# A hybrid RG-LRU/S5 decoder layer on one core: one PSUM bank is skipped behind the gates of the LRU stage

## Chip, core and metric

The kernel runs on one core of one Trainium2 chip. The metric is device time in microseconds (us), the median of the runs shown; lower is better. Beside it stands one profiled execution, from which all durations below come. The engines are named as in the profile: PE is TensorE, ACT is ScalarE, DVE is VectorE, POOL is GpSimd, SP issues the DMAs.

## The reference, cut to what matters

One layer works on 1024 prompt positions and 8 sequences of 4 sample positions, 1056 columns in all, with 1024 features. The part around the change is the recurrent branch:

```python
z = u @ w_in + b_in
z_lru, z_gate, z_s5, m_a, m_b = jnp.split(z, SPLITS, axis=-1)
v, conv_new = causal_conv(z_lru, conv0, w_conv, b_conv)
...
g = jnp.einsum('bthi,ghij->gbthj', vb, w_gates).reshape(2, Bn, T, D_RNN)
gates = jax.nn.sigmoid(g.astype(jnp.float32) + b_gates.astype(jnp.float32)[:, None, None, :])
r, i = gates[0], gates[1]
log_a = -LRU_C * r * jax.nn.softplus(-lam.astype(jnp.float32))
a = jnp.exp(log_a)
bterm = jnp.sqrt(-jnp.expm1(2.0 * log_a)) * (i * v.astype(jnp.float32))
_, h = lax.associative_scan(_lin_op, (a, bterm), axis=1)
br_a = (h.astype(dt) * jax.nn.gelu(z_gate)) @ w_lru_out
```

Before it lie the conditioning (ada) and the S5 branch, behind it the weight GLU, the output product, two layer norms and a SwiGLU.

## The kernel before

Activations are held with features on the 128 partitions and the 1056 columns in three blocks of 352. Every float32 product is made of three TensorE products of rounded high and low halves (high by high, high by low, low by high), so one block of 128 output features over 1024 inputs is 24 matmuls. The order of the work is written out by hand: each engine executes its instructions in the order in which the code issues them, and `later(n, fn)` puts a step n blocks (`tick()`) further on.

**The LRU stage** is the loop `for j in range(8)` behind `conv_bias()`. I call its iterations passes. Pass j does, on PE, in this order:

- block 0 of z_lru for feature tile j (`zl_block(w, j, 0)`, matmul line L997),
- from pass 1 on, the gates of tile j-1 (`lru_gates`, matmul line L1043): six outputs, for each of three blocks one for gate r and one for gate i, three matmuls each,
- blocks 1 and 2 of z_lru for tile j (L997),
- three blocks of z_gate for tile j-1 (`product(... zg_evac)`, matmul line L344),
- one part of the ada product (`ada_job`, L403) and, after each fourth part, its small selecting product (`ada_sel4`, L413).

Each result leaves PSUM as follows. A z_lru block is scaled by ACT (L1002) and then read three more times by DVE, which adds the other three taps of the convolution straight from PSUM (L126, `scalar_tensor_tensor`). A gate leaves by one ACT tanh (L1044). A z_gate block leaves by two ACT instructions (L1034, L1035).

The rest of the recurrence runs on DVE, ACT and POOL beside the products: `lru_0` to `lru_3` (tanh L1050, exp L1051, sqrt L1057 on ACT; the scan L1071 on DVE), `lru_out` (gelu with the tanh L1080 on ACT), the split into high and low halves of v (`lru_split`: ACT L1027, DVE L117) and of the result (`lru_hi_lo`: ACT L1086, POOL L117). A pass of ACT begins, in this document, with the L1027 of block 2: it waits for DVE's sample convolution (`lru_conv`).

**The banks.** PSUM has eight banks of 512 columns. In this stage `banks[0]` is 7: bank 7 is kept for the ada product, and `bank()` hands out the other seven in turn:

```python
    def bank():
        b = bank_at[0] % banks[0]
        bank_at[0] += 1
        return ps[:, b]
```

A pass takes twelve: block 0 of z_lru, six gates, blocks 1 and 2 of z_lru, three blocks of z_gate. If block 0 has bank s, the gates have s+1 to s+6, and block 1 is given s again: a product into a bank begins when the last reader of what it held is done. Block 2 is given the first gate's bank, and the z_gate blocks those of gates 2, 3 and 4.

After the loop come the last gates in the same way: one block of the last merge gate (`blocks(w, e, 0, 1)`), the gates of tile 7, an `ada_job`, three blocks of z_gate for tile 7 (the first one in the bank of that merge block), and two more merge blocks. The following stages, which open with `lr.close()`, load their operands anew and go on with the same turn of seven banks, later six.

Of the kernel before, what the change touches and what calls it, by code (L numbers as in the profile page):

```python
# [71 lines left out]
def tile_hawk_s5(ctx: ExitStack, tc: tile.TileContext, io):  # L72
# [46 lines left out]
    def ts(e, out, a, s0, s1=None, op0=OP.mult, op1=OP.add):  # L119
        if s1 is None:  # L120
            e.tensor_scalar(out, a, s0, None, op0=op0)
        else:
            e.tensor_scalar(out, a, s0, s1, op0=op0, op1=op1)

    def stt(e, out, a, s, b, op0, op1):
        e.scalar_tensor_tensor(out, a, s, b, op0=op0, op1=op1)  # L126
# [68 lines left out]
# [4 lines that stand above are left out]
# [839 lines left out]
    def lru_gates(j):  # L1038
        for nb in range(3):
            for g, dst in ((0, t_e), (1, t_f)):  # L1040
                b = bank()
                for q, (w, v) in enumerate(((gwh, vhr), (gwl, vhr), (gwh, vlr))):
                    PE.matmul(b[:, :NB], w[:, g, :], v[:, nb], start=q == 0, stop=q == 2)  # L1043
                A.activation(dst[:, 352 * nb:352 * nb + 352], b[:, :NB], AF.Tanh,  # L1044
                             bias=bgh[:, g, j:j + 1], scale=0.5)

    def lru_0(j):

        stt(V, t_f, t_f, 1.0, t_bb[j % 2], OP.add, OP.mult)
        A.activation(t_c, t_e, AF.Tanh, bias=sp2[:, j:j + 1], scale=sp2[:, j:j + 1])  # L1050
        A.activation(t_e, t_e, AF.Exp, bias=sp4[:, j:j + 1], scale=sp4[:, j:j + 1])  # L1051
        ts(V, t_e, t_e, 1.0, op0=OP.add)
# [43 lines left out]
    def gates_and_on(j):  # L1096
        lru_gates(j)
        for n, fn in ((1, lru_0), (2, lru_1), (3, lru_2), (5, lru_3)):
            later(n, fn, j)
        if j < 7:  # L1100
            later(2, gate_split, j + 1)
# [831 lines left out]
```

## Time and profile before

| | |
|---|---|
| time, median of 3 runs | 1794.03 us (1792.05 to 1795.2) |
| the profiled execution's own time | 1794.15 us |
| its span, first to last instruction | 1792.4 us |
| PE busy | 1719.7 us, 96% of the span |
| DVE busy | 1101.9 us, 61% |
| POOL busy | 882.0 us, 49% |
| ACT busy | 716.2 us, 40% |
| mean granted clock of TensorE | 0.982 of full speed |

How to read it: time and span differ by 1.75 us, which lie around the first and the last instruction. A busy share is an average over stages of different kinds; PE's idle time is spread over a few places, and the view of waits names them. The LRU stage runs from about 358 to about 640 us of the span. "idle before <-releaser" is the time that an engine stood still before an instruction and the line whose end let it go on. [...]

### The profile page before, as it was taken

The numbers are of one execution on the slowest core, as the hardware profiler recorded it, in microseconds if no ns is written. First come the engines' busy times: TensorE is split into PE (matmuls) and PEld (weight loads), VectorE is DVE, ScalarE is ACT, GpSimd is POOL, SyncE is SP. The second block draws the span as 40 slices with busy tenths as digits, with TensorE's granted clock in tenths as the row PEclk, the third lists the DMA queues.
The fourth block names the chain that finished last, engine by engine and source line by source line (L and its number), as shares of the span: only waits on it lengthen the run. The fifth ranks groups of instructions, "written<-read, shape, count | busy, mean of one in ns | idle before, by whom it ended". The sixth has DMA issues, their size and how long they took to land.

```text
span 1792.4 us, 33919 instructions
## 1 busy us (share of the span) xinstructions
PE 1719.7 (96%) x13380; PEld 1685.8 (94%) x13380; DVE 1101.9 (61%) x2026; ACT 716.2 (40%) x1456; POOL 882.0 (49%) x744
## 2 busy tenths in 40 slices
PE   6999999999898999999999998999999999999996
PEld 5989999998898999999999998999999998999996
DVE  6989999457687733322785685345554454533587
ACT  4533334346556633223354364344433333211244
POOL 3454343124344322355678616577767775222654
PEclk9999999999899999999999999999999999999999
DMA  9345555431112168665344323333322236832211
GB/s 358 89 123 154 177 152 168 132 106 63 50 42 74 36 183 241 220 224 188 113 155 158 111 96 118 108 124 120 116 96 96 102 115 250 335 125 76 81 37 61
DMA packets 118639, 240.93 MB, mean 134 GB/s; under 512 B 23120, under 2 KB 62288, under 8 KB 115408
## 3 DMA queue, kind: packets, MB, share of 16 engines
q1 hardware_dynamic: 118480, 238.76, 40.7%
q8 instruction: 105, 1.72, 0.4%
q14 instruction: 54, 0.44, 0.1%
HBM read 179.59 MB, written 54.97 MB: 131 GB/s over the span
## 4 chain that ended last, share of the span: by engine, by line
PE 76%; DVE 12%; DMA 4%; ACT 4%; POOL 3%; issue 2%; SPq 1%; POOLq 0%; DVEq 0%; ACTq 0%
PE ps L1206 36%; PE ps L344 19%; PE ps L1725 12%; PE ps L997 4%; DVE lru_t L126 3%; DVE rear_t L117 2%; DVE r_t L117 1%; DMA x_in_t<-in_x_dram 1%; POOL r_t L117 1%; POOL weights_t L117 1%; DVE lru_t L117 1%; DMA small_t<-in_w_down_dram 1%; DMA ada_w_t<-in_w_ada_dram 1%; DVE s_t L117 1%; PE ps L752 1%
## 5 line engine op out<-in xcount | busy, mean ns | idle before, releaser
L1206 PE MATMUL ps<-r_t,weights_t 128*128 128x264 f32 x5496 | 683.2, 285 | 10.9 <-POOL weights_t L117 7.4
L1206 PEld LDWEIGHTS ps<-r_t,weights_t 128*128 128x128 f32 x5496 | 672.5, 188 | 17.2 <-POOL weights_t L117 9.3
L117 POOL TENSOR_TENSOR weights_t<-small_t,weights_t 128x512 fp32r<-128x512 f32 (+3 forms) x312 | 390.8, 1268 | 494.7 <-ACT weights_t L232 436.8
L344 PE MATMUL ps<-r_t,weights_t 128*128 128x352 f32 x2808 | 469.7, 326 | 2.7 <-ACT weights_t L232 1.5
L344 PEld LDWEIGHTS ps<-r_t,weights_t 128*128 128x128 f32 x2808 | 453.2, 190 | 10.5 <-issue 6.1
L232 ACT ACTIVATE weights_t<-small_t 128x512 fp32r<-128x512 f32 (+3 forms) x286 | 151.5, 572 | 247.1 <-PE ps L1725 99.0
L1725 PE MATMUL ps<-r_t,weights_t 128*128 128x264 f32 x1344 | 166.6, 286 | 3.7 <-ACT weights_t L232 3.4
L1725 PEld LDWEIGHTS ps<-r_t,weights_t 128*128 128x128 f32 x1344 | 165.3, 190 | 4.9 <-ACT weights_t L232 3.6
L126 DVE SCALAR_TENSOR_TENSOR rear_t<-ps,small_t,rear_t 128x264 f32<-128x264 f32 (+1 forms) x192 | 92.4, 482 | 123.1 <-PE ps L1725 96.0
L117 DVE TENSOR_TENSOR small_t<-ps,small_t 128x264 f32<-128x264 f32 (+1 forms) x228 | 84.7, 378 | 102.0 <-ACT small_t L1650 74.4
L126 DVE SCALAR_TENSOR_TENSOR rear_t<-rear_t,ps 128x264 f32<-128x264 f32 (+1 forms) x74 | 33.1, 456 | 176.1 <-PE ps L1206 98.3
L997 PE MATMUL ps<-r_t,weights_t 128*128 128x356 f32 (+1 forms) x576 | 110.2, 356 | 21.3 <-DVE lru_t L126 21.3
L997 PEld LDWEIGHTS ps<-r_t,weights_t 128*128 128x128 f32 x576 | 106.2, 213 | 24.2 <-ACT lru_t L1050 22.7
L117 POOL TENSOR_TENSOR r_t<-rear_t,r_t 128x264 fp32r<-128x264 f32 (+2 forms) x77 | 96.7, 1259 | 60.9 <-ACT r_t L1221 24.1
L117 DVE TENSOR_TENSOR rear_t<-rear_t,small_t 128x32 f32<-128x32 f32 (+3 forms) x137 | 95.7, 707 | 41.0 <-POOL weights_t L117 30.9
L117 POOL TENSOR_TENSOR rear_t<-rear_t,small_t 128x264 f32<-128x264 f32 (+1 forms) x108 | 91.0, 865 | 54.6 <-ACT small_t L1269 44.3
L117 POOL TENSOR_TENSOR weights_t<-rear_t,weights_t 128x512 fp32r<-128x512 f32 x57 | 75.2, 1324 | 55.6 <-ACT weights_t L1566 55.5
L1725 PE MATMUL ps<-r_t 128*128 128x264 f32 x768 | 96.7, 286 | 0.8 <-POOL r_t L117 0.8
L1725 PEld LDWEIGHTS ps<-r_t 128*128 128x128 f32 x768 | 94.6, 188 | 1.7 <-POOL r_t L117 1.2
L117 POOL TENSOR_TENSOR r_t<-small_t,r_t 128x528 fp32r<-128x528 f32 (+1 forms) x58 | 78.7, 1368 | 35.3 <-ACT r_t L211 25.3
L117 DVE TENSOR_TENSOR s_t<-s_t 128x128 f32<-128x128 f32 (+4 forms) x184 | 74.7, 449 | 5.6 <-ACT s_t L700 3.2
L1206 PE MATMUL ps<-r_t 128*128 128x264 f32 x600 | 76.7, 283 | 0.0
(228 smaller groups left out, 1944.3 us busy)
## 6 DMA issues: line engine op xcount, KB each, us to landing
d_f<-r_t SPq DMA_DIRECT2D x44, 528.0 KB
r_t<-d_f SPq DMA_DIRECT2D x22, 1056.0 KB
small_t<-in_w_up_dram SPq DMA_DIRECT2D x43, 512.0 KB
small_t<-in_w_in_dram SPq DMA_DIRECT2D x40, 512.0 KB
small_t<-in_w_ada_dram SPq DMA_DIRECT2D x32, 512.0 KB
small_t<-in_w_glu_dram SPq DMA_DIRECT2D x32, 512.0 KB
ada_w_t<-in_w_ada_dram SPq DMA_DIRECT2D x16, 512.0 KB
small_t<-in_w_out_dram SPq DMA_DIRECT2D x16, 512.0 KB
```

Of the source, the lines that this page charges most:

```text
L117: e.tensor_tensor(out, a, b, op=op)
L126: e.scalar_tensor_tensor(out, a, s, b, op0=op0, op1=op1)
L232: A.activation(self.hi[:, s], self.raw[:, s], AF.Copy)
L344: PE.matmul(out[:, :NB], a[:, k, :], x[:, h, nb, k, :], start=bool(first and n == 0 and q == 0), stop=bool(last and n == len(kts) - 1 and ...
L752: PE.matmul(wb_[64 * h:64 * h + 64, 136 * n:136 * n + 136], wt[:, 2 * pr + h, 64 * r:64 * r + 64], ub[:, 2 * pr + h, 8:144], start=True, s ...
L997: PE.matmul(b[:, 4 - n:356], a[:, k, :], r1w[:, h, k, 352 * nb - n:352 * nb + 352], start=k == q == 0, stop=k == 7 and q == 2)
L1206: PE.matmul(out[:, :Q], a[:, k, :], x(h, k), start=bool(first and n == 0 and q == 0), stop=bool(last and n == len(kts) - 1 and q == 2), sk ...
L1725: PE.matmul(b[:, :Q], a[:, n, :], f[:, h, Q * q:Q * q + Q], start=n == i == 0, stop=k == k1 - 1 and i == 2)
```

## The change

One call is added at the end of `lru_gates`: a bank is taken from the turn and not used.

```diff
@@ -1044,6 +1044,8 @@
                 A.activation(dst[:, 352 * nb:352 * nb + 352], b[:, :NB], AF.Tanh,
                              bias=bgh[:, g, j:j + 1], scale=0.5)
 
+        bank()
+
     def lru_0(j):
```

No instruction is added, removed or moved on any engine; what changes is which bank an instruction writes and reads, and so what it waits for. `lru_gates` is called eight times. With block 0 of z_lru in bank s and the gates in s+1 to s+6, block 1 now has s+1 (the first gate's), block 2 s+2 (the second gate's), and the z_gate blocks those of gates 3, 4 and 5. The next pass begins at s+6, and its first gate takes s, the bank in which block 0 of the pass before stood.

PE, in pass 1 to 7 of the LRU stage, from the last gate's matmuls (L1043) to the second z_lru block (L997 with 356 columns); in brackets the engines whose semaphores an instruction waits for:

```order
 L1043 MATMUL ps<-r_t,lru_w_t 128x352 [waits Activation_49]
 L1043 MATMUL ps<-r_t,lru_w_t 128x352 x2
-L997 MATMUL ps<-r_t,weights_t 128x356 [waits DVE_49,Activation_49]
+L997 MATMUL ps<-r_t,weights_t 128x356 [waits Activation_49]
 L997 MATMUL ps<-r_t,weights_t 128x356 x23
 L997 MATMUL ps<-r_t,weights_t 128x356 [waits Activation_49]
```

The first matmul of block 1 no longer waits for DVE; it still waits for ACT.

PE again, in passes 2 and later, at the step from block 0 of z_lru to the first two gates:

```order
 L997 MATMUL ps<-r_t,weights_t 128x352 [waits Pool_49]
 L997 MATMUL ps<-r_t,weights_t 128x352 x9
-L1043 MATMUL ps<-r_t,lru_w_t 128x352
-L1043 MATMUL ps<-r_t,lru_w_t 128x352 [waits DVE_49]
+L1043 MATMUL ps<-r_t,lru_w_t 128x352 [waits DVE_49] x2
 L1043 MATMUL ps<-r_t,lru_w_t 128x352 x4
 L1043 MATMUL ps<-r_t,lru_w_t 128x352 [waits DVE_49,Activation_49]
```

The first gate's first matmul now waits for DVE's reads of block 0 of the pass before; it waited for nothing there.

## Rows read from the trace of the kernel before

**Rows 1.** View of waits of PE (us in total, times, longest us).
```profile
PE ps L997 <- DVE lru_t L126: 21.3, 6, 3.9
```

**Rows 2.** Windows: us, busy time (x instructions) by engine, PEclk, DMA share, GB/s.
```profile
381.76:408.58 26.82, 26.82 (x182) 26.34 (x178) 17.60 (x26) 15.79 (x30) 7.97 (x9) 1.00 0.24 85
...
385.69:396.45 10.76, 10.76 (x68) 10.70 (x67) 6.86 (x11) 8.18 (x12) 0.00 (x0) 1.00 0.27 111
412.51:427.51 15.00, 12.52 (x67) 12.26 (x67) 10.10 (x12) 9.36 (x14) 4.43 (x3) 0.89 0.15 48
443.57:460.68 17.11, 13.36 (x68) 13.10 (x67) 10.20 (x13) 10.39 (x15) 7.02 (x6) 0.80 0.12 36
476.74:494.42 17.68, 13.80 (x69) 13.71 (x69) 10.41 (x14) 10.54 (x15) 6.00 (x6) 0.81 0.11 36
510.48:526.66 16.18, 12.46 (x67) 12.19 (x67) 10.16 (x13) 10.36 (x15) 6.98 (x6) 0.89 0.12 39
542.72:559.75 17.03, 13.29 (x67) 13.03 (x67) 10.19 (x13) 10.38 (x15) 7.00 (x6) 0.80 0.12 39
575.81:593.31 17.50, 13.75 (x69) 13.49 (x67) 10.20 (x13) 10.38 (x15) 7.02 (x6) 0.80 0.12 36
```

**Rows 3.** Timeline of PE, passes 1, 3, 4 (start, us, engine, line, operation).
```profile
385.69 3.04 PE L1043 MATMUL ps<-r_t,lru_w_t 128*128 128x352 f32 x18
388.57 8.04 PE L997 MATMUL ps<-r_t,weights_t 128*128 128x356 f32 x48
...
443.57 3.04 PE L1043 MATMUL ps<-r_t,lru_w_t 128*128 128x352 f32 x18
450.37 10.47 PE L997 MATMUL ps<-r_t,weights_t 128*128 128x356 f32 x48 [3.75 <-DVE lru_t L126]
...
479.62 0.31 PE L413 MATMUL ps<-small_t 128*128 128x36 f32 x2
```

**Rows 4.** Windows, as in rows 2: behind a wait in pass 3, and behind LRU.
```profile
450.30:453.00 2.70, 2.63 (x9) 2.66 (x10) 1.91 (x3) 0.88 (x1) 0.00 (x0) 0.50 0.00 0
...
656.00:660.00 4.00, 2.87 (x16) 2.30 (x16) 0.00 (x0) 3.44 (x5) 2.54 (x2) 1.00 1.08 269
```

**Rows 5.** Timeline of ACT, DVE and POOL, from pass 3 to pass 4.
```profile
439.23 0.50 ACT L1027 ACTIVATE r_t<-lru_t 128x352 fp32r<-128x352 f32 x1 [5.14 <-DVE lru_t L126]
...
445.38 2.77 ACT L1044 ACTIVATE lru_t<-ps,small_t 128x352 f32<-128x352 f32 x6
...
448.42 1.80 DVE L126 SCALAR_TENSOR_TENSOR lru_t<-ps,small_t,lru_t 128x349 f32<-128x349 f32 x3
...
449.91 1.27 ACT L1051 ACTIVATE lru_t<-lru_t,small_t 128x1056 f32<-128x1056 f32 x1
...
450.34 1.25 DVE L126 SCALAR_TENSOR_TENSOR lru_t<-lru_t 128x1056 f32<-128x1056 f32 x1
...
451.51 0.70 DVE L121 TENSOR_SCALAR lru_t<-lru_t 128x1056 f32<-128x1056 f32 x1
456.95 0.65 ACT L1002 ACTIVATE lru_t<-ps,small_t 128x352 f32<-128x352 f32 x1 [5.77 <-PE ps L997]
...
457.63 1.83 DVE L126 SCALAR_TENSOR_TENSOR lru_t<-ps,small_t,lru_t 128x352 f32<-128x352 f32 x3 [5.42 <-ACT lru_t L1002]
...
458.65 2.47 POOL L117 TENSOR_TENSOR r_t<-lru_t,r_t 128x1056 fp32r<-128x1056 f32 x1 [10.09 <-ACT r_t L1086]
459.37 2.13 DVE L117 TENSOR_TENSOR r_t<-lru_t,r_t 128x352 fp32r<-128x352 f32 x1
...
472.38 0.50 ACT L1027 ACTIVATE r_t<-lru_t 128x352 fp32r<-128x352 f32 x1 [5.13 <-DVE lru_t L126]
```

**Rows 6.** Timeline of ACT, PE and DVE behind the loop.
```profile
611.05 2.77 ACT L1044 ACTIVATE lru_t<-ps,small_t 128x352 f32<-128x352 f32 x6
...
612.14 4.08 PE L344 MATMUL ps<-r_t,weights_t 128*128 128x352 f32 x24
...
632.79 0.53 DVE L126 SCALAR_TENSOR_TENSOR lru_t<-lru_t 128x352 f32<-128x352 f32 x1 [3.96 <-ACT lru_t L1080]
```

## The prediction

> **What bounds the kernel now.** I read the view of waits first. TensorE is busy almost throughout, so what matters is where it stands still. The largest entry is this stage's: matmuls of line 997 waited six times for DVE's line 126, 21.3 us in all, the longest wait 3.9 us [rows 1]. Line 997 is z_lru and line 126, with PSUM as a source, is the convolution: block 1 waits for the bank that DVE still reads block 0 from.
>
> Then I read the stage pass by pass, as windows from the first gate matmul to the first z_gate matmul, a stretch in which PE does the same 66 matmuls each time (18 of gates, 48 of z_lru). Pass 1 needs 10.76 us at full clock, passes 2 to 7 need 15.00 to 17.68 us [rows 2]. In the timeline of PE, pass 1 goes from its gates to block 1 in 2.88 us (385.69 to 388.57), pass 3 in 6.80 us (443.57 to 450.37), of which 3.75 us are the wait [rows 3]. The second loss is the clock. [...]
>
> Last I read the other engines in pass 3. DVE reads block 0 from 448.42 to 450.22 and PE starts block 1 at 450.37 [rows 3, 5]: the wait ends exactly there. The first gate's bank was free much earlier: the six gate tanhs begin at 445.38 and take 2.77 us, so the first ends at about 445.84 [rows 5].
>
> **What the change removes.** Block 1 of z_lru gets the bank of the first gate, and its first matmul loses its wait for DVE. PE can begin block 1 at 443.57 + 2.88 = 446.45, and in pass 3 the first gate's bank is free 0.6 us before that. So the wait goes, and with it the stop that precedes the low clock. The excess of each stretch over pass 1 is 4.24, 6.35, 6.92, 5.42, 6.27 and 6.74 us; 0.31 us of the third is the selecting product in that stretch [rows 2, 3], which stays. The sum is 35.6 us. Of it 21.3 us is idle time by the view of waits; the other 14.3 us is mostly matmuls at the lower clock. Pass 1 has nothing to lose, since DVE has no gelu of an earlier tile to do there.
>
> The other waits of the edit I cost at nothing. Block 2 takes the second gate's bank and the z_gate blocks those of gates 3 to 5. All six tanhs end at 448.15 [rows 5], over 2 us before block 2 could begin (446.45 + 4.0 = 450.5, with half of the 8.04 us of the two blocks [rows 3]). The first gate of a pass now waits for DVE's reads of block 0 of the pass before; in pass 3 they end at 450.22 and the gates of pass 4 start at 476.74 [rows 2, 5]. In the later stages only the phase of the turn moves, and their banks are reused in the same order. No DMA and no order changes.
>
> **What it adds.** PE's pass becomes 26.82 us [rows 2], and something else may no longer keep up. The chain through DVE and ACT goes round once a pass too: from ACT's first instruction of pass 3 to that of pass 4, 472.38 - 439.23 = 33.15 us [rows 5]. Part of that round is today's wait for PE: DVE ends lru_0 at 451.51 + 0.70 = 452.21 and stands still until block 1 arrives, at 457.63. With block 1 done at about 450.5, ACT can evict it as soon as its exp ends (449.91 + 1.27 = 451.18, and 0.65 us for the eviction), so DVE starts on it at 452.21, 5.42 us earlier. The round is then 33.15 - 5.42 = 27.7 us. It may be 0.3 us less: DVE's split of block 0 takes 2.13 us and ends 0.4 us after POOL's 2.47 us (458.65 to 461.12), and POOL starts 1.02 us after DVE's taps now, about 0.7 us after them when ACT has gone straight on. So the round is 27.4 to 27.7 us against PE's 26.8.
>
> So DVE and ACT fall behind by 0.6 to 0.9 us a pass, and PE meets it where its margin is least, at the first gate's eviction, the bank of block 1. I take pass 3 to begin with the margin of today, 0.6 us, since in pass 2 PE and the chain lose about the same stretch. Pass 4 has 0.0 to -0.3 us left, and its selecting product of 0.31 us covers that. Pass 5 waits 0.3 to 0.9 us, passes 6 and 7 what the round is too long, 0.6 to 0.9 us each. Behind the loop there is one such place more: the first z_gate block of tile 7 takes the first gate's bank, free at 611.05 + 0.46 = 611.51 and wanted at 612.14 [rows 6]; the lag makes it wait 0.7 to 1.0 us. The sum of the new waits is 2.2 to 3.7 us. Below, nothing is possible, if DVE and ACT run a little closer; I take 3.0 us, in the middle of the two, since the rows do not tell which of the two rounds holds. I charge no clock for these waits: at 656 to 660 us PE stood still for over a microsecond (2.87 us busy of 4.00) and the granted clock stayed at 1.00 [rows 4]. If each of the four did cost a slow stretch, its price is today's: the excess of a pass less its wait, at most 6.74 - 3.75 = 3.0 us, 12 us for four.
>
> What is late next, once this is gone, is the end of the stage on DVE: the last tile's gelu. There DVE waits 3.96 us for ACT before 632.79 us [rows 6], for merge blocks that PE itself has to produce first, so a lag of 1 to 2 us disappears. The loads of the next stage start when this one closes and move forward with it. I count the whole gain as reaching the end.
>
> **Sum.** 1794.15 (the profiled execution's own time, 0.1 us from the median 1794.03) - 35.6 + 3.0 = 1761.5 us.
>
> **Rivals.**
>
> - The wait goes and no new one comes: 1794.15 - 35.6 = 1758.5 us. For it: the 27.4 us round is near PE's 26.8, and part of DVE's stops beside POOL may fall otherwise.
> - The waits become short, but the clock still falls behind them: 1794.15 - 21.3 + 3.0 = 1775.9 us. Against it: the window at 656 to 660 us [rows 4], where the clock held. [...]
> - Slower. With PE no longer waiting, DVE's and POOL's work fall onto each other in another way, and the round of DVE and ACT grows instead of shrinking. It decides from a round longer than the 33.15 us of now [rows 5]; at 34 us the six passes lose 5 us and the time is 1799 us. For it: the split of block 0 takes 2.13 us beside POOL [rows 5]. Against it: 27.7 us would have to grow by 5.4 us, and the order of each engine's work does not change, so that DVE and POOL keep most of their places to each other.
> - The change does not do what it says, because something else in block 1 waits as long: 1794 us. Against it: its first matmul has only ACT left to wait for, and in pass 3 the six tanhs were done 2.2 us before block 1 began.
>
> **How the numbers follow.** My forecast, waits of 1.5 us to 6 us (1760 to 1764.5), has 0.62; no new waits 0.16; the clock rival with all between it and the forecast 0.15; no effect 0.03; slower 0.02; 0.02 is left for a later stage that takes something back or gives more. The range has to hold 8 in 10: I reach down to 1756 (1758.5 less the 2 us by which the runs scatter) and up to 1772, most of the way to the clock rival and near the 12 us bound. A measurement of this kernel tells about 0.2% (3.6 us) from no change: faster 0.95, within 0.03, slower 0.02.
>
> **What would show it.** Right: the wait of line 997 for DVE's line 126 gone from PE's waits; windows from first gate to first z_gate matmul near 10.8 us (11.1 in pass 4, up to 11.7 in passes 5 to 7) at a clock of 1.00; new small waits of line 997 for ACT's line 1044, under 1 us each; DVE's wait for block 1 gone and the round from one L1027 of block 2 to the next 27.4 to 27.7 us in passes 4 to 7. Wrong: such windows of over 13 us, a clock below 0.95 in them, a round above 29 us, or a gain in this stage that does not reach the end of the span.

## The result, and the profile after

| | before | after |
|---|---|---|
| median time | 1793.55 us (1792.05 to 1795.2, 4 runs) | 1760.55 us (1759.51 to 1761.71, 4 runs) |
| ratio | | 0.9819, 95% interval 0.9807 to 0.9831 |
| span of the profiled execution | 1792.4 us | 1757.7 us |
| PE / DVE busy | 1719.7 / 1101.9 us | 1704.9 / 1102.5 us |
| mean granted clock of TensorE (PEclk in the windows), share of full speed | 0.982 | 0.992 |

The forecast was 1761.5 us. (The kernel before has a fourth run here, hence 1793.55 us and not 1794.03.) DVE's work is the same; PE is busy for 15 us less with the same matmuls, and stands still for less.

The view of waits after the change, PE, 355 to 610 us (us in total, times, longest us). The entry of 21.3 us [rows 1] is gone:

```profile
PE ps L997 <- ACT lru_t L1044: 0.8, 3, 0.3
PE ps L344 <- ACT lru_t L1044: 0.4, 1, 0.4
```

The windows that answer to those of before [rows 2], from the first gate matmul to the first z_gate matmul of passes 1 to 7, after the change:

```profile
384.74:395.47 10.73, 10.73 (x67) 10.73 (x67) 6.85 (x11) 8.18 (x12) 0.00 (x0) 1.00 0.27 107
411.53:422.26 10.73, 10.73 (x67) 10.73 (x67) 10.11 (x12) 9.38 (x14) 4.44 (x3) 1.00 0.20 71
438.32:449.06 10.74, 10.74 (x69) 10.74 (x67) 9.26 (x13) 10.19 (x15) 6.52 (x6) 1.00 0.20 61
465.12:476.17 11.05, 11.05 (x70) 11.05 (x70) 9.40 (x13) 10.39 (x15) 5.54 (x6) 1.00 0.18 62
492.23:503.58 11.35, 11.03 (x68) 10.73 (x67) 9.87 (x13) 10.79 (x15) 7.13 (x6) 1.00 0.20 59
519.64:530.86 11.22, 11.00 (x68) 10.71 (x67) 9.74 (x13) 10.66 (x15) 7.00 (x6) 1.00 0.18 61
546.92:558.16 11.24, 10.98 (x67) 10.69 (x67) 9.76 (x13) 10.69 (x15) 7.03 (x6) 1.00 0.20 63
```

The granted clock is 1.00 in all seven, and passes 2 to 7 are within 0.62 us of pass 1. The timeline of ACT, DVE and POOL in pass 3, to hold against the one of before [rows 5]:

```profile
433.96 0.50 ACT L1027 ACTIVATE r_t<-lru_t 128x352 fp32r<-128x352 f32 x1 [5.13 <-DVE lru_t L126]
...
443.17 1.80 DVE L126 SCALAR_TENSOR_TENSOR lru_t<-ps,small_t,lru_t 128x349 f32<-128x349 f32 x3
...
445.85 0.63 ACT L1002 ACTIVATE lru_t<-ps,small_t 128x352 f32<-128x352 f32 x1
446.25 0.70 DVE L121 TENSOR_SCALAR lru_t<-lru_t 128x1056 f32<-128x1056 f32 x1
...
446.87 1.82 DVE L126 SCALAR_TENSOR_TENSOR lru_t<-ps,small_t,lru_t 128x352 f32<-128x352 f32 x3
...
447.53 2.48 POOL L117 TENSOR_TENSOR r_t<-lru_t,r_t 128x1056 fp32r<-128x1056 f32 x1 [4.22 <-ACT r_t L1088]
...
448.61 1.78 DVE L117 TENSOR_TENSOR r_t<-lru_t,r_t 128x352 fp32r<-128x352 f32 x1
...
461.28 0.50 ACT L1027 ACTIVATE r_t<-lru_t 128x352 fp32r<-128x352 f32 x1 [5.14 <-DVE lru_t L126]
```

DVE reads block 0 until 444.97, but PE began block 1 at 441.20 (438.32 + 2.88). DVE goes from lru_0 (446.25 + 0.70) to block 1 without a stop, where it stood still for 5.42 us [rows 5], and the round from one L1027 of block 2 to the next is 461.28 - 433.96 = 27.3 us instead of 33.15.

Two lines of PE before and two after bound the LRU stage, from its first z_lru block to the first block of the next product:

```profile
357.98 11.81 PE L997 MATMUL ps<-r_t,weights_t 128*128 128x352 f32 x72
...
640.01 11.71 PE L344 MATMUL ps<-r_t,weights_t 128*128 128x352 f32 x72
```

```profile
357.03 11.81 PE L997 MATMUL ps<-r_t,weights_t 128*128 128x352 f32 x72
...
605.23 11.72 PE L344 MATMUL ps<-r_t,weights_t 128*128 128x352 f32 x72
```

The stage took 282.0 us and takes 248.2: 33.8 us of the 34.7 us by which the span is shorter. The rest lies ahead of the stage (357.98 against 357.03), where nothing was changed; in the other runs' traces the stage begins between 356.75 and 359.04 us. Behind it both have 1152.4 to 1152.5 us left, so nothing is given back.

### The profile page after: what moved, and what is told of

It reads as the page before. It is cut to its first block, busy times and chain, and to the rows that moved or that the text cites. A ratio compares the mean times of both kernels' runs of the same rounds, so it can differ in the third digit from the quotient of the medians.

```text
span 1757.7 us, 33905 instructions
## 1 busy us (share of the span) xinstructions
PE 1704.9 (97%) x13380; PEld 1671.8 (95%) x13380; DVE 1102.5 (63%) x2026; ACT 715.3 (41%) x1456; POOL 883.9 (50%) x744
## 4 chain that ended last, share of the span: by engine, by line
PE 75%; DVE 13%; ACT 4%; POOL 3%; DMA 2%; issue 2%; SPq 0%; POOLq 0%; DVEq 0%; ACTq 0%
PE ps L1208 38%; PE ps L344 19%; PE ps L1727 12%; DVE lru_t L126 4%; PE ps L997 2%; DVE rear_t L117 1%; POOL weights_t L117 1%; POOL r_t L117 1%; DVE lru_t L117 1%; DVE r_t L117 1%; DVE s_t L117 1%; PE ps L752 1%; PE ps L822 1%; PE ps L821 1%; PE ps L403 1%
## 5 line engine op out<-in xcount | busy, mean ns | idle before, releaser
L1208 PEld LDWEIGHTS ps<-r_t,weights_t 128*128 128x128 f32 x5496 | 672.6, 188 | 16.8 <-POOL weights_t L117 10.5
L997 PE MATMUL ps<-r_t,weights_t 128*128 128x356 f32 (+1 forms) x576 | 97.0, 326 | 0.8 <-ACT lru_t L1044 0.8
L997 PEld LDWEIGHTS ps<-r_t,weights_t 128*128 128x128 f32 x576 | 93.2, 188 | 3.1 <-ACT lru_t L1044 1.7
```

Source lines behind the costliest of these rows:

```text
L997: PE.matmul(b[:, 4 - n:356], a[:, k, :], r1w[:, h, k, 352 * nb - n:352 * nb + 352], start=k == q == 0, stop=k == 7 and q == 2)
L1208: PE.matmul(out[:, :Q], a[:, k, :], x(h, k), start=bool(first and n == 0 and q == 0), stop=bool(last and n == len(kts) - 1 and q == 2), sk ...
```

## Experiments

Ratios are to the kernel before on the same chip, with their 95% interval. The change, experiments 1 to 4, 5 to 8, and 9 with 10 were measured in four sittings. The median of the kernel before moved by 2 us between them (from 1793.55 to 1791.46), so in experiments 4 to 8 a time set against the change's is good to that; experiments 9 and 10 are from one sitting.

**1. The same skip at another place.** From the kernel before:

```diff
         w = use_w("in", j)
+        if j:
+            bank()
         zl_block(w, j, 0)
...
+    bank()
     blocks(w, e, 0, 1)
     gates_and_on(7)
```

> From the kernel before, with the same eight skipped banks, but each one ahead of block 0 of z_lru (passes 1 to 7 and the merge block behind the loop) instead of behind the gates. The turn moves on as in the change, yet block 1 is back in block 0's bank. Theory (what counts is whose bank block 1 takes): no change, 1793.5 us within 3 us, line 997 waits 21 us for DVE's line 126, stretches from first gate to z_gate of 15 to 17.7 us. Rival (a turn of other length helps by itself, here or in the later stages): near 1760 us.

Measured: 1793.0 us, ratio 1.0006 (0.9997 to 1.0015). The wait of line 997 is that of before to a tenth:

```profile
PE ps L997 <- DVE lru_t L126: 21.3, 6, 3.9
```

A turn that moves on by thirteen does nothing by itself; a bank has to be skipped between the gates and block 1.

**2. The skip in four of seven passes.** From the change:

```diff
-        bank()
+        if j < 4:
+            bank()
```

> The change, but the bank is skipped only in passes 1 to 4 (gates of tiles 0 to 3). Theory (each pass has its own loss): passes 2 to 4 give back 4.2 + 6.4 + 6.6 = 17.2 us, passes 5 to 7 keep theirs, and the first of them waits about 0.9 us longer because DVE has fallen behind: 1777 us. Rival (one wait pushes DVE back for the rest of the loop, or the gain comes from the end of the loop): near 1760 or near 1793 us.

Measured: 1777.5 us, ratio 0.9916 (0.9901 to 0.9930). Windows of passes 5, 6, 7, and of pass 3:

```profile
494.18:511.25 17.07, 12.31 (x68) 12.05 (x67) 11.19 (x13) 11.40 (x15) 7.96 (x6) 0.90 0.12 37
527.31:543.59 16.28, 12.53 (x67) 12.27 (x67) 10.18 (x13) 10.38 (x15) 7.00 (x6) 0.90 0.12 40
559.65:575.87 16.22, 12.46 (x67) 12.20 (x67) 10.19 (x13) 10.38 (x15) 7.01 (x6) 0.89 0.12 38
440.33:451.06 10.73, 10.73 (x67) 10.73 (x67) 9.24 (x13) 10.18 (x15) 6.52 (x6) 1.00 0.20 60
```

Each pass loses for itself. The first one without the skip waits 4.75 us, about 0.9 us more than the others had before, which fits the lag of DVE behind PE that the expectation had put at that size.

**3. The wait filled with matmuls.** From the kernel before, behind the gates (`b0` is the first gate's bank):

```diff
+        for _ in range((0, 16, 23, 23, 23, 23, 23, 0)[j]):
+            PE.matmul(b0[:, :NB], gwh[:, 0, :], vhr[:, 0], start=True, stop=True)
```

> From the kernel before, without the skip: in passes 2 to 7, PE does 16 (pass 2) or 23 more matmuls behind the gates, into the first gate's bank, which nobody reads; they fill the time in which it waits for DVE. The wait stays as long, but PE does not stand still. Theory (14 us of the 35.6 are the low clock that follows the stop): stretches of 13.4 to 14.7 us at a granted clock of 1.00, time 1793.5 - 14 = 1779.5 us, within 2 us. Rival (the matmuls behind the wait are slow for another reason, such as DVE and ACT at work on PSUM): clock still 0.8 to 0.9 or matmuls still slow, 1793 us or more.

Measured: 1779.7 us, ratio 0.9931 (0.9917 to 0.9946). Windows of passes 2 and 3, and PE in pass 3:

```profile
411.74:425.12 13.38, 13.38 (x83) 13.26 (x83) 10.12 (x12) 9.37 (x14) 4.44 (x3) 1.00 0.17 56
441.18:455.88 14.70, 14.70 (x91) 14.42 (x90) 10.21 (x13) 10.38 (x15) 7.03 (x6) 1.00 0.17 60
```

```profile
444.06 3.84 PE L1049 MATMUL ps<-r_t,lru_w_t 128*128 128x352 f32 x23
447.90 8.15 PE L997 MATMUL ps<-r_t,weights_t 128*128 128x356 f32 x48
```

The 48 matmuls of blocks 1 and 2 take 8.15 us behind the filled wait, where they took 10.47 behind the empty one [rows 3], with ACT and DVE as busy as before, and the granted clock is 1.00 in both windows, where it was 0.89 and 0.80 [rows 2]. So the 35.6 us come apart: about 13 us was the low clock behind the stop, and some 22 us the stop, which the added matmuls only cover. More work on PE made the kernel 12.6 us faster.

**4. Block 1 in the last gate's bank.** From the change:

```diff
-        bank()
+        for _ in range(6):
+            bank()
```

> The change with six banks skipped instead of one: block 1 takes the last gate's bank, which ACT frees 2.3 us after the first gate's. Theory (block 1 begins when its bank is evicted, and PE and the round of DVE and ACT then hold each other up): pass 1 and 2 wait 0.8 to 0.9 us, pass 3 1.7 us, passes 4 to 7 about 1.2 us each, the end of the loop 2 to 3 us; 9 us more than the change, 1769.5 us, if the clock holds. If the clock falls behind such short waits, up to 3 us more for each, 1785 us. Rival (any bank that DVE does not read does as well): 1760.5 us.

Measured: 1770.4 us, ratio 0.9882 (0.9866 to 0.9899), 9.9 us more than the change (10.5 us between the two profiled executions). Waits of PE and the window of pass 6:

```profile
PE ps L997 <- ACT lru_t L1044: 9.1, 7, 1.6
PE ps L344 <- ACT lru_t L1044: 1.7, 1, 1.7
```

```profile
526.00:538.55 12.55, 10.98 (x68) 10.69 (x68) 10.19 (x13) 10.37 (x15) 7.01 (x6) 1.00 0.17 53
```

Which bank block 1 takes matters even among those that ACT alone reads. Passes 4 to 7 waited 1.5 to 1.6 us, more than the 1.2 us expected, and passes 1 to 3 and the end of the loop less; the sum was 1 to 1.5 us off. The clock held, at 1.00 in all seven windows.

**5. One DVE instruction less.** From the change, `ts(V, t_e, t_e, 1.0, op0=OP.add)` left out of `lru_0`.

> The change, with one DVE instruction of 0.7 us a pass left out (the addition of 1 to the exponential in lru_0, so the recurrence is computed with another factor). Theory (the waits that are left come from the round of DVE and ACT, 27.3 us against PE's 26.8): the round falls below 26.8 us, line 997 waits no longer for ACT's line 1044 in passes 5 to 7, stretches of 10.7 us (11.05 in pass 4), some 1.5 us less in the stage, 1759 us. Rival (they come from the fixed order of ACT's evictions): the waits stay at 0.2 to 0.4 us.

Measured: 1761.5 us, ratio 0.9832 (0.9813 to 0.9852), and the same waits for line 1044 (0.8 us, 3 times). My theory fell here: the round stayed at 27.3 us. POOL and DVE in pass 4:

```profile
477.00 2.46 POOL L117 TENSOR_TENSOR r_t<-lru_t,r_t 128x1056 fp32r<-128x1056 f32 x1 [5.50 <-ACT r_t L1087]
...
477.72 2.13 DVE L117 TENSOR_TENSOR r_t<-lru_t,r_t 128x352 fp32r<-128x352 f32 x1
```

DVE comes to its split of block 0 about 0.5 us earlier in the round, and the split takes 2.13 us again; it ends 0.39 us after POOL's instruction, as it did at 2.13 us before [rows 5] and at 1.78 us in the change (448.61 to 450.39, POOL's end at 450.01). So the round runs not through DVE's own work there but through ACT (exp, eviction of block 1, high half of the result) and POOL. The rival of this run, ACT's fixed order of evictions, would leave the waits as well; experiment 9 decides between the two.

**6 and 7. One and two DVE instructions more.** From the change, the first instruction of `lru_1` issued twice, and three times:

```diff
         stt(V, t_d, t_c, -1.0, t_e, OP.add, OP.mult)
+        stt(V, t_d, t_c, -1.0, t_e, OP.add, OP.mult)
```

> The change, with one DVE instruction more in each lru_1 (its first one issued twice, 1.25 us). Theory (with the wait for block 0's bank gone, DVE and ACT have no room left): the round becomes 28.6 us, PE waits some 1.5 to 1.8 us in each of passes 3 to 7 and 2 us at the end for the first gate's bank; 7 to 8 us more than the change, 1768 us, with the clock at 1.00 if stops of under 2 us leave it alone, up to 1785 us if not. Rival (DVE, 63% busy, still has slack): 1760.5 us.

> As the run before with two such instructions, 2.5 us a pass. Theory: the round becomes 29.8 us and PE waits about 3 us a pass from pass 3 on; 16 us more than the change, 1777 us, if the clock holds. In the kernel before, stops of 2.5 to 3.9 us were followed by the low clock, so I expect it here too, at 1.5 to 3 us for each of six stops: 1786 to 1795 us. Rival (DVE has slack): 1760.5 us.

Measured: 1768.2 us, ratio 0.9871 (0.9854 to 0.9887), and 1781.3 us, ratio 0.9943 (0.9928 to 0.9958). The windows of pass 6, first with one more and then with two:

```profile
524.23:536.77 12.54, 10.99 (x68) 10.70 (x67) 11.06 (x14) 11.99 (x18) 7.09 (x6) 1.00 0.16 56
```

```profile
533.34:547.80 14.46, 12.52 (x68) 12.23 (x67) 12.78 (x14) 12.96 (x19) 7.98 (x6) 0.88 0.14 48
```

PE's waits and the start of pass 6's block 1 with two more:

```profile
PE ps L997 <- ACT lru_t L1044: 10.9, 6, 2.8
```

```profile
538.32 9.64 PE L997 MATMUL ps<-r_t,weights_t 128*128 128x356 f32 x48 [1.94 <-ACT lru_t L1044]
```

and ACT's eviction of that block:

```profile
544.07 0.65 ACT L1002 ACTIVATE lru_t<-ps,small_t 128x352 f32<-128x352 f32 x1 [0.53 <-PE ps L997]
```

The work that is added 1.25 us a pass behind the split shows in full (round 28.6 us), so DVE has no room left there although it is busy for 63% of the span. With two more the clock falls as well, to a mean of 0.88 in the window of pass 6. The time stayed under the 1786 to 1795 us of the expectation, although the round was 30.5 us and not 29.8. PE's matmuls of blocks 1 and 2 took 1.5 us more a pass. Part of that went into the round, about 0.7 us: ACT now waits 0.53 us for block 1, and DVE's split takes 2.12 us instead of 1.78. The rest came out of PE's waits, 1.9 us in passes 4 to 7 where about 3 us were expected. So here stops and slow matmuls did not simply add up.

**8. The addition on POOL.** From the change, `ts(P, ...)` in place of `ts(V, ...)` in `lru_0`.

> The change, with the addition of 1 in lru_0 done by POOL instead of DVE, a version that might be better than both kernels. Theory: DVE's part of the round is 0.6 us shorter, but POOL's split of the result starts later and holds up DVE's split of block 0 longer; the round comes to 26.9 to 27.4 us and the stage gains 0 to 1.5 us: 1759 to 1760.5 us, no difference that can be measured. Rival (POOL's work falls onto more of DVE's instructions): round over 28 us, 1765 us.

Measured: 1766.2 us, ratio 0.9858 (0.9839 to 0.9878): the rival. POOL and DVE in pass 5:

```profile
503.56 3.06 POOL L121 TENSOR_SCALAR lru_t<-lru_t 128x1056 f32<-128x1056 f32 x1 [2.72 <-ACT lru_t L1053]
...
505.77 0.52 DVE L117 TENSOR_TENSOR r_t<-lru_t,r_t 128x352 fp32r<-128x352 f32 x1
...
506.60 2.48 POOL L117 TENSOR_TENSOR r_t<-lru_t,r_t 128x1056 fp32r<-128x1056 f32 x1
506.66 3.54 DVE L126 SCALAR_TENSOR_TENSOR lru_t<-lru_t 128x1056 f32<-128x1056 f32 x1 [0.37 <-POOL lru_t L121]
```

What takes DVE 0.70 us took POOL 3.06 us, and POOL's part of the split came behind it. DVE's split of block 0 no longer met it and took 0.52 us. The first instruction of `lru_1` met it in its place: it waited 0.37 us for POOL's addition and then took 3.54 us beside POOL's part of the split, where it took 1.25 us in the change (at 450.31), with POOL idle. The round grew to 28.4 us.

**9 and 10. POOL's part made shorter, and the change again beside it.** From the change:

```diff
-            later(3 if j < 7 else 2, lru_hi_lo, j - 1, 0, 3, P)
+            later(3 if j < 7 else 2, lru_hi_lo, j - 1, 0, 1, P)
+            later(3 if j < 7 else 2, lru_hi_lo, j - 1, 1, 2, V)
```

> The change, with the low half of the result (lru_hi_lo in passes 1 to 7) shared: POOL does one block of three, DVE the other two (about 0.9 us more on DVE), so that POOL is done before DVE comes to its split of block 0. Theory (the round of 27.3 us runs through ACT's exp, eviction and high half, then POOL's 2.47 us, behind which DVE's split ends): the split takes 0.5 us instead of 1.7, the round falls to about 26.9 us, the waits for line 1044 in passes 5 to 7 to at most 0.1 us, and the time to about 1759 us, 1 us less than the change, which is at the edge of what can be told. Rival (the round is set by DVE's own work): 0.9 us more a pass, round 28.2 us, 1766 us.

> The change itself, beside the run before on the same chip. Both theories: as measured, ratio 0.982, round 27.3 us, 1758 to 1761 us.

Measured: 1758.8 us (1757.42 to 1758.79, 5 runs), ratio 0.9812 (0.9798 to 0.9826), against 1760.7 us (1760.01 to 1761.34, 4 runs), ratio 0.9823 (0.9809 to 0.9837). With the shared split, the window of pass 6, and the timeline of POOL and DVE in pass 4 and of ACT from pass 6 to pass 7:

```profile
518.68:529.41 10.73, 10.73 (x67) 10.73 (x67) 9.61 (x13) 9.90 (x15) 5.47 (x4) 1.00 0.19 63
```

```profile
473.21 0.95 POOL L117 TENSOR_TENSOR r_t<-lru_t,r_t 128x352 fp32r<-128x352 f32 x1 [5.09 <-DVE lru_t L121]
...
474.80 1.32 DVE L117 TENSOR_TENSOR r_t<-lru_t,r_t 128x704 fp32r<-128x704 f32 x2
...
513.84 0.50 ACT L1027 ACTIVATE r_t<-lru_t 128x352 fp32r<-128x352 f32 x1 [5.13 <-DVE lru_t L126]
...
540.67 0.50 ACT L1027 ACTIVATE r_t<-lru_t 128x352 fp32r<-128x352 f32 x1 [5.12 <-DVE lru_t L126]
```

The round is 26.8 us, which is PE's own pass, and line 997 waits for nothing in the stage. Although DVE does more, its two instructions (the low half of two blocks and the split) take 1.32 us, where the split alone took 1.78. The runs of this version and of the change do not overlap, but the intervals of the ratios do; the 2 us agree with the 2.1 us of waits that went. It is the fastest of these kernels. ACT evicts in the same order as in the change, so the rival of experiment 5 is out.

## Why the prediction was right

- **The wait.** It was put down to the bank of block 0. Right: it went when block 1 got another bank, and not when the turn moved elsewhere (experiment 1).
- **35.6 us removed.** Right: all six stretches came to the length of pass 1 but for the new waits, and 33.8 us came out of the stage. That the part beyond 21.3 us was the clock was an estimate from the rows: after the stop of 3.75 us in pass 3 the granted clock was 0.50, and the windows of passes 2 to 7 had 0.80 to 0.89 where pass 1 had 1.00 [rows 2, 3, 4]. Experiment 3 shows it, with 13 us for the 14.3 us of the estimate.
- **New waits, 3.0 us of 2.2 to 3.7.** Their place was right, passes 5 to 7 and the tile behind the loop, for the first gate's bank. Their size was just under the range: against pass 1, passes 5 to 7 have 0.62, 0.49 and 0.51 us more, and the last z_gate product starts 0.44 us later behind its gates than before; 2.1 us in all. The view of waits has 1.2 us of this; the rest lies beside it. A wait counts from the end of the last gate matmul, 3.04 us behind the start of the first, while block 1 without a wait starts 2.88 us behind it [rows 3], and behind the waits the 48 matmuls take 8.11 to 8.15 us instead of 8.02. The term that was mis-sized is the round. I bounded it by 27.4 and 27.7 us and took the middle, "since the rows do not tell which of the two rounds holds". They did tell: DVE's split ended 0.4 us after POOL's instruction [rows 5], and it is POOL's end that sets the round, 27.3 us, within 0.1 us of the lower bound. I had made the end of lru_0 on DVE the point at which the round goes on; experiment 5 takes 0.7 us from it and nothing moves.
- **No clock for the new waits.** Right, at 0.2 to 0.4 us each. The window that I rested this on [rows 4] shows less than I read in it: its "over a microsecond" is two stops, of 0.35 and 0.77 us, and I expected waits of up to 1.0 us. The experiments fill this gap: waits of 0.64 to 1.62 us, in four to seven passes of a kernel, left the clock at 1.00 in their windows (experiments 4, 6 and 8), and waits of 1.90 to 2.84 us were followed by a lower one, 0.85 to 0.89 in theirs (experiment 7). For the rival at 1775.9 us, a low clock behind waits as short as these, no run speaks: the clock is 1.00 in all seven windows of the change. The two stops between 656 and 660 us, in the kernel before:

```profile
656.66 0.59 PE L344 MATMUL ps<-r_t,weights_t 128*128 128x352 f32 x2 [0.35 <-ACT weights_t L232]
658.03 7.71 PE L344 MATMUL ps<-r_t,weights_t 128*128 128x352 f32 x46 [0.77 <-POOL weights_t L117]
```

- **The rival on the slower side.** DVE's and POOL's collisions are real (DVE's split took 1.67 to 2.13 us beside POOL's in the change, 0.52 us with POOL idle), but the order of the work kept them where they were. Experiment 8 is what that rival looks like: POOL's work fell on another instruction of DVE, the round became 1.1 us longer, and PE paid in each pass from pass 4 on.
- **Nothing given back.** Right: 1152.4 and 1152.5 us behind the stage.
- **The number.** That 1761.5 us came within 1 us of the median is in part luck. The stage gave 33.8 us where 35.6 - 3.0 = 32.6 us were forecast, the profiled execution gained another 0.95 us ahead of the stage, and the four runs of each kernel lie 2 to 3 us apart.

## What to carry to other kernels

Where buffers are handed out in turn, look at who reads the one that comes next, and how late that reader's engine is: a product that follows short, quickly evicted ones should take one of their buffers and not that of a long reader. A stop of TensorE can cost more than its length: in experiment 7 the window of pass 6, with a stop of 1.94 us, took 14.46 us, and without a stop, in experiment 9, 10.73 us. So price a wait with the matmuls behind it. And once PE no longer waits, follow the round of the other engines through every engine it touches, POOL too, before calling an engine free because it is busy for 63% of the time.

## What the runs showed of the hardware

- Of the 19 stops of 0.64 to 1.66 us in this stage (eight in experiment 4, six in experiment 6, five in experiment 8), 17 lie in windows with a granted clock of 1.00; behind the other two (1.66 us in experiment 4, 1.47 us in experiment 8) 24 matmuls took 4.08 and 4.09 us, against 4.08 us without a stop [rows 6]. The six of 1.90 to 2.84 us in experiment 7 lie in windows of 0.85 to 0.89, the three of 3.75 to 4.75 us in experiment 2 in windows of 0.89 to 0.90, and the six of 2.48 to 3.88 us in the kernel before in windows of 0.80 to 0.89 [rows 2], with 0.50 in one that holds only matmuls behind the stop of pass 3 [rows 4]. In experiment 1 the 48 matmuls behind its six stops of 2.47 to 3.88 us took 9.58 to 10.83 us, against 8.05 us in pass 1, without a stop.
- DVE's 352-column split took 0.52 us with POOL idle (at 395.13 in the kernel before). Beside POOL's split of 2.45 to 2.48 us, in six passes each of the kernel before and of the change, it took 1.67 to 2.13 us: it started 0.71 to 1.18 us after POOL's and ended 0.37 to 0.39 us after it. A DVE instruction on 1056 columns that took 1.25 us with POOL idle took 3.54 us beside POOL's split in experiment 8 and ended 1.1 us after it. Beside POOL's TENSOR_SCALAR of 3.06 us in the same run, DVE's split took 0.52 us.
